# A two-layer decoder trunk: the input and the small weights handed over in the layout that the opening uses

## The chip, the cores and the metric

The kernel runs on one core of one Trainium2 chip. The metric is the device time of one execution in microseconds, as the median of several runs. The core has a matmul engine (TensorE, PE in the profile, with its weight loads shown as PEld), VectorE (DVE), ScalarE (ACT), GpSimd (POOL) and SyncE (SP). Transfers are issued from SyncE's queue, from ScalarE's and from GpSimd's, and run on 16 DMA engines.

## The reference, cut to what matters

The input is x of 512 tokens by 1024 features. Two mixer layers follow each other, each with a dense SwiGLU network behind it, and a last norm. The change touches the first mixer alone:

```python
hn = rmsnorm(h, mix_norm_g[0])                  # h is x at this point
z = gelu(hn @ w_in)                             # 1024 -> 2048
u, v = split(z, 2)
v = layernorm(v, ln_g, ln_b)                    # 4 chunks of 128 tokens, 8 groups of 128 features
w = where(causal, w_s, 0)                       # (8, 128, 128): group, target token, source token
mixed = einsum('gts,bcsgd->bctgd', w, v) + b_s
h = h + (u * mixed) @ w_out
```

All is float32. The later parts (first feed-forward network, retention, second network) are the same before and after.

## The kernel before

**Products.** A float32 value is split into a high part rounded to fp32r (ScalarE, a copy) and the low rest (VectorE, a subtraction); a product of two matrices is three fp32r matmuls (high by high, high by low, low by high), accumulated in PSUM. Most large products use seven block products instead of eight (`seven`), named P1, P7, P6, Q4, P5, P2 and P3, on sums of weight blocks and sums of activation blocks. A sum of weight blocks is made either by VectorE from two loaded tiles, or by a DMA that adds while it loads (issued by POOL); which blocks go which way is set by the arguments `dma` and `onto`.

**The opening** (lines 1407 to 1476). The left operand of a matmul has the features on the partitions, but x is stored by token. So each of eight pieces of x (128 tokens by 512 features, `load_x`) is loaded into X, turned by four TensorE transposes into PSUM (`turn_in`, lines 1265 to 1291), scaled there by the norm weight of its feature by VectorE into `xr_in`, copied to its high part `XH_in` by ScalarE and reduced to its low part `XL_in` by VectorE. The factor of the norm that depends on the token (`rc`) is put in later, where v is activated, and into R for u. The norm weights are loaded as 8 rows of 128 (`load_rows`) and turned by a transpose into a column per block (`rows_to_cols`). The first half of v's columns (`ps_v`, 96 products of 128x512) is multiplied piece by piece as the turned pieces appear (`open_step`); the weights come through `open_w`. The squares for the norm are summed by ScalarE over X.

Before that TensorE runs five wake-up matmuls on ones (`WAKE`), and a few more (`fill`) after the first turned pieces.

**The rest of the first mixer.** The second half of v's columns (`project_n("v1", ...)`, also `ps_v`), then u by seven block products in the order `UO`, among which the spatial mixing (`mix`, fp32 matmuls) is put. The spatial weights are loaded target first (`wsn`), turned by eight transposes (`wsT`), copied by VectorE and masked by POOL (`prepare_mix`, lines 1573 to 1581). Their row sums come from two fp32 matmuls with a tile of ones (`prepare_bias`, lines 1583 to 1589). The gains of the layer norm and of retention are 32 rows, turned by one transpose (`gains_ps`). The product by w_out (`so`) adds into X, and the first network (`gu`, `dn`) follows.

**Order.** No engine's order is that of the program text. Every operation is recorded with an estimated duration; a planner gives each a due time, worked back from the matmuls that need it (`backward`, `rec.ahead` moves it earlier), then simulates all engines and DMA queues forward and lets each engine take the ready operation that is due first, TensorE the ready matmul that was recorded first (`forward`). The operations are then issued in the simulated order, and each engine keeps to it. Tiles come from 39 buffers of 4 KB a partition (`G`) and eight PSUM banks. As all operations are issued by one line (377) of the recorder, the profile is read by tiles.

Of the kernel before, what the change touches and what calls it, by code (L numbers as in the profile page):

```python
# [8 lines left out]
F32 = mybir.dt.float32  # L9
# [14 lines left out]
GROUPS = 8  # L24
WAKE = 5
PREP = 5
# [10 lines left out]
U_DMA = ("P7",)  # L37
U_ONTO = ()
TABLES_AHEAD = 120000
# [630 lines left out]
@with_exitstack  # L670
def trunk(ctx, tc, x, positions, mix_g, ffn_g, fin_g, sgu_w_in, sgu_w_s, sgu_b_s, sgu_ln_g, sgu_ln_b,
          sgu_w_out, ret_w_in, ret_gn_g, ret_w_out, ffn_w_gu, ffn_w_down, invf, decay, out):
    rec = Recorder(tc)
# [83 lines left out]
    def rows_to_cols(name):
        n = rows_in[name].shape[0]
        ps = PS(f"{name}_ps", (P, 1, T))
        nc.tensor.transpose(ps[:, 0, 0:n], rows_in[name], ident[0:n, 0:n])  # L760
        cols = const.tile([P, n], F32, name=f"{name}_cols")
        nc.vector.tensor_copy(cols, ps[:, 0, 0:n])
        done(ps)
        return cols


# [495 lines left out]

    turned = {}

    def turn_in(c, j):

        ps = PS(f"xT_in_{c}_{j}", (P, 4, P))
        for k in range(4):
            turned[c, j] = nc.tensor.transpose(ps[:, k, :], X[:, c, (4 * j + k) * P:(4 * j + k + 1) * P], ident)
        if (c, j) == (0, 0):  # L1270
            xn.update(name="in", h=XT("XH_in"), l=XT("XL_in"))
        if c % 2 == 0:
            XR.setdefault(("in", c // 2), []).append(G(f"xr_in_{c // 2}_{j}", F32, (P, 4, H)))
        cs = slice(c * P, (c + 1) * P)
        for k0, n in ((0, 2), (2, 2)) if (c, j) == (0, 0) else ((0, 4),):
            ks, js = slice(k0, k0 + n), slice(4 * j + k0, 4 * j + k0 + n)
            own = XR["in", c // 2][j][:, ks, (c % 2) * P:(c % 2 + 1) * P]
            if (c, j, k0) == (0, 0, 0):
                rec.ahead = 4000
            if (c, j, k0) == (0, 0, 2):  # L1280
                for k in range(2):
                    nc.scalar.activation(own[:, k, :], ps[:, 2 + k, :], AF.Copy, scale=mix0[:, 2 + k:3 + k])
            else:
                nc.vector.tensor_tensor(own, ps[:, ks, :], mix0[:, js, None].to_broadcast([P, n, P]), ALU.mult)
            if (c, j, k0) == (0, 0, 0):
                nc.vector.tensor_copy(xn["h"][:, js, cs], own)
            else:
                nc.scalar.activation(xn["h"][:, js, cs], own, AF.Copy)
            rec.ahead = 0
            nc.vector.tensor_tensor(xn["l"][:, js, cs], own, f32(xn["h"][:, js, cs]), ALU.subtract)  # L1290
        done(ps)

    def normed(name, g, more=None):
# [122 lines left out]

    rec.ahead = 6000
    load_rows(nc.scalar, "mix0", mix_g[0:1])
    load_x(0, 0)
    load_x(1, 0)  # L1420
    rec.ahead = 0
    mix0 = rows_to_cols("mix0")
    v0w, v0r = [None] * NC, [None] * NC

    def open_w(i):
        wr = G(f"wr_v0_{i}")
        for a in range(2) if i < 2 else ():
            nc.sync.dma_start(wr[:, a, :], w_in[(2 * i + a) * P:(2 * i + a + 1) * P, D:D + T])
        if i >= 2:
            nc.sync.dma_start(wr, w_in[2 * i * P:(2 * i + 2) * P, D:D + T].rearrange("(a p) n -> p a n", p=P))  # L1430
        wh, wl = G(f"wh_v0_{i}", F32R), G(f"wl_v0_{i}", F32R)
        for at in (slice(0, 1), slice(1, 2)) if i < 2 else (slice(0, 2),):
            nc.scalar.activation(wh[:, at, :], wr[:, at, :], AF.Copy)
            nc.vector.tensor_tensor(wl[:, at, :], wr[:, at, :], f32(wh[:, at, :]), ALU.subtract)
        v0w[i] = wh, wl

    def open_step(c, i):
        wh, wl = v0w[i]
        cs = slice(c * P, (c + 1) * P)
        o = vps[c // 2][:, c % 2, :]  # L1440
        for n, (x_, w_) in enumerate((("h", wh), ("h", wl), ("l", wh))):
            for a in range(2):
                k = 2 * i + a
                nc.tensor.matmul(o, xn[x_][:, k, cs], w_[:, a, :], start=(k == 0 and n == 0), stop=(k == KD - 1 and n == 2),
                                 skip_group_check=True)

    turn_in(0, 0)
    vps = [PS(f"ps_v0_{i}") for i in range(2)]

    def fill(n, at):  # L1450
        for _ in range(n):
            rec.follow(nc.tensor.matmul(vps[1][:, 0, :], flat[:, 0, 0:P], flat[:, 0, :], start=True, stop=True), turned[at])

    fill(2, (0, 0))
    for j in range(2):
        for c in range(NC):
            if c == 0:
                open_w(2 * j)
            if (c, j) != (3, 1):
                at = (c + 1) % NC, j + (c + 1) // NC  # L1460
                if at != (1, 0):
                    load_x(*at)
            if c == 1:
                open_w(2 * j + 1)
            if (c, j) != (3, 1):
                turn_in(*at)
            if (c, j) == (0, 0):
                fill(1, at)
            open_step(c, 2 * j)
            if c == 1:  # L1470
                open_step(0, 2 * j + 1)
            if c >= 1:
                open_step(c, 2 * j + 1)
            if j == 1:
                square_in(c)
    rc = rsqrt_cols(ss2, NC, 1.0 / D, "n0")
# [72 lines left out]


    load_rows(nc.sync, "gains", ret_gn_g, sgu_ln_g, sgu_ln_b)
    gains = rows_to_cols("gains")

# [13 lines left out]
    add_b = G("add_b", F32, (P, GROUPS, P))  # L1567
    wsn = G("wsn", F32, (P, GROUPS, P))
    nc.sync.dma_start(wsn, sgu_w_s[0].rearrange("g t s -> t g s"))
    nc.sync.dma_start(add_b, sgu_b_s.rearrange("l g t -> l (g t)").to_broadcast([P, GROUPS * P]))  # L1570
    R = TMP("R0")

    def prepare_mix():
        ps = PS("wsT", (P, GROUPS, P))
        for g in range(GROUPS):
            nc.tensor.transpose(ps[:, g, :], wsn[:, g, :], ident)
        nc.vector.tensor_copy(wst, ps)
        done(ps)
        nc.gpsimd.affine_select(
            out=wst, in_=wst, compare_op=ALU.is_ge, fill=0.0, base=0,  # L1580
            pattern=[[0, GROUPS], [1, P]], channel_multiplier=-1)

    def prepare_bias():
        ps = PS("rowsum", (P, GROUPS, P))
        for j in range(2):
# [25 lines left out]

    project_n("v1", w_in, ((D + T, T),), after_v1)
    mx = [None] * KD
# [36 lines left out]
    def mix(j, half):  # L1650
        for i in (2 * half, 2 * half + 1):
# [10 lines left out]
            if i % 2 == 1:  # L1662
                done(ps)

    jobs.extend(seven("u", w_in, rows(0, KD), 0, T, uparts, gate_u,
                      {("P1", 0): prepare_bias, ("P1", 1): lambda: mix(0, 0), ("P7", 0): lambda: mix(0, 1), ("P7", 1): lambda: mix(1, 0),
# [317 lines left out]
```

## Time and profile before

| | |
|---|---|
| median of 3 runs | 1176.3 us (1176.13 to 1176.56) |
| profiled execution | 1176.45 us, span 1174.5 us |
| granted clock | 0.999 |
| PE / PEld busy | 1165.5 / 1063.8 us (99% / 91%) |
| DVE / ACT / POOL busy | 1008.8 / 695.3 / 177.5 us (86% / 59% / 15%) |
| DMA | 233.00 MB, mean 198 GB/s |

Times are microseconds from the start of the span. In a row of the timeline or the chain stand start, duration, engine, line, operation, the tile written, the tiles read and the count; in brackets the idle time before it and what ended it. A row of the waits says who waited for whom, the sum, how often and the longest. The busy time of matmuls overlaps, since they are pipelined; the distance between starts is what one costs in a stream. A row of the landing times gives the size of a load and the time from issue to landing. A row that groups instructions ends with busy time and the mean of one in ns.

### The profile page before, as it was taken

What the parts mean: (1) busy time and instruction counts of PE and PEld (TensorE: products, weight loads), DVE (VectorE), ACT (ScalarE), POOL (GpSimd) and SP (SyncE); (2) the same over time, 40 slices, a digit from 0 to 9 for tenths busy, and PEclk for the clock granted to TensorE, in tenths of its full rate; (3) what the DMA queues carried; (4) which work ended last, traced back from release to release, by engine and by line L of the source; (5) the groups of instructions that cost most, each with busy time, mean ns of one, the idle gap of its engine ahead of it and who ended that gap; (6) DMA issues with size and microseconds to landing.
All of it is one profiled execution on the core that took longest, in us unless ns stands there. A gap on an engine that the chain in (4) does not pass through costs nothing.

```text
span 1174.5 us, 18866 instructions
## 1 busy us (share of the span) xinstructions
PE 1165.5 (99%) x7492; PEld 1063.8 (91%) x7492; DVE 1008.8 (86%) x1246; ACT 695.3 (59%) x915; POOL 177.5 (15%) x153
## 2 busy tenths in 40 slices
PE   9999999999999999999999999999999999999997
PEld 7899899989999988888889898888999889999986
DVE  7999999798779899998868787899998987665896
ACT  7446876456543558767555585577675544535474
POOL 0012121211100220221111111220211111001220
PEclk9999999999999999999999999999999999999999
DMA  9458988899856898988777678887897898769892
GB/s 327 120 143 191 319 202 207 180 239 217 201 141 158 193 189 264 220 184 209 179 175 193 148 193 215 189 170 252 212 220 169 202 241 198 189 153 247 179 224 82
DMA packets 132777, 233.00 MB, mean 198 GB/s; under 512 B 7592, under 2 KB 32208, under 8 KB 132688
## 3 DMA queue, kind: packets, MB, share of 16 engines
q1 hardware_dynamic: 91152, 156.80, 40.8%
q0 software_dynamic: 41376, 74.72, 38.2%
q8 instruction: 59, 0.97, 0.3%
q10 hardware_dynamic: 160, 0.27, 0.1%
q14 instruction: 30, 0.25, 0.1%
HBM read 228.61 MB, written 2.10 MB: 196 GB/s over the span
## 4 chain that ended last, share of the span: by engine, by line
PE 98%; ACT 1%; DMA 0%; DVE 0%; SPq 0%; issue 0%; DVEq 0%
PE X_gu L377 22%; PE Y_gu L377 11%; PE X_dn L377 9%; PE X_vg L377 7%; PE Z_gu L377 5%; PE Y_dn L377 5%; PE X_qk L377 4%; PE ps_v L377 4%; PE Y_vg L377 4%; PE X_ro L377 4%; PE Z_dn L377 3%; PE pv L377 2%; PE Y_qk L377 2%; PE X_u L377 2%; PE X_so L377 2%; PE Y_ro L377 2%
## 5 line engine op out<-in xcount | busy, mean ns | idle before, releaser
L377 ACT ACTIVATE wh_gu_P<-wr_gu_P 128x1024 fp32r<-128x1024 f32 x132 | 138.6, 1061 | 119.9 <-DMA wr_gu_P<-in_ffn_w_gu 32.8
L377 DVE TENSOR_TENSOR wl_gu_P<-wr_gu_P,wh_gu_P 128x1024 fp32r<-128x1024 f32 x132 | 160.2, 1222 | 42.5 <-ACT wh_gu_P L377 29.8
L377 POOL DMA_DIRECT2D wr_gu_P<-in_ffn_w_gu x50 | 60.7, 1248 | 378.4 <-DVE wl_gu_P L377 186.0
L377 ACT ACTIVATE wh_dn_P<-wr_dn_P 128x1024 fp32r<-128x1024 f32 (+1 forms) x72 | 69.4, 984 | 44.1 <-PE Y_gu L377 12.4
L377 DVE TENSOR_TENSOR wl_dn_P<-wr_dn_P,wh_dn_P 128x1024 fp32r<-128x1024 f32 (+1 forms) x72 | 80.5, 1134 | 11.0 <-ACT wh_dn_P L377 10.6
L377 POOL DMA_DIRECT2D wr_dn_P<-in_ffn_w_down x40 | 46.3, 1203 | 172.8 <-DVE wl_dn_P L377 63.7
L377 DVE TENSOR_TENSOR wl_vg_P<-wr_vg_P,wh_vg_P 128x1024 fp32r<-128x1024 f32 x48 | 57.6, 1221 | 8.7 <-ACT wh_vg_P L377 6.3
L377 ACT ACTIVATE wh_vg_P<-wr_vg_P 128x1024 fp32r<-128x1024 f32 x48 | 49.7, 1057 | 9.5 <-PE Z_qk L377 3.5
L377 POOL DMA_DIRECT2D wr_vg_P<-in_ret_w_in x26 | 31.6, 1292 | 140.3 <-DVE wl_vg_P L377 60.4
L377 PE MATMUL Z_gu<-XH_f,wh_gu_P 128*128 128x256 f32 x176 | 50.0, 284 | 0.0
L377 PE MATMUL X_gu<-XH_f,wh_gu_P 128*128 128x256 f32 x176 | 49.9, 284 | 0.0
L377 PE MATMUL Y_gu<-xP7h_f,wh_gu_P 128*128 128x256 f32 x176 | 49.8, 283 | 0.0
L377 PE MATMUL Y_gu<-xP7l_f,wh_gu_P 128*128 128x256 f32 x176 | 49.8, 283 | 0.0
L377 PE MATMUL Y_gu<-xP7h_f,wl_gu_P 128*128 128x256 f32 x176 | 49.8, 283 | 0.0
L377 PE MATMUL X_gu<-xP6h_f,wh_gu_P 128*128 128x256 f32 x176 | 49.8, 283 | 0.0
L377 PE MATMUL X_gu<-xP6l_f,wh_gu_P 128*128 128x256 f32 x176 | 49.8, 283 | 0.0
L377 PE MATMUL X_gu<-xP6h_f,wl_gu_P 128*128 128x256 f32 x176 | 49.8, 283 | 0.0
L377 PE MATMUL X_gu<-xP5h_f,wh_gu_P 128*128 128x256 f32 x176 | 49.8, 283 | 0.0
L377 PE MATMUL X_gu<-xP5l_f,wh_gu_P 128*128 128x256 f32 x176 | 49.8, 283 | 0.0
L377 PE MATMUL X_gu<-xP5h_f,wl_gu_P 128*128 128x256 f32 x176 | 49.8, 283 | 0.0
L377 PE MATMUL Y_gu<-XH_f,wh_gu_Q 128*128 128x256 f32 x176 | 49.8, 283 | 0.0
L377 PE MATMUL Y_gu<-XL_f,wh_gu_Q 128*128 128x256 f32 x176 | 49.8, 283 | 0.0
(676 smaller groups left out, 4388.1 us busy)
## 6 DMA issues: line engine op xcount, KB each, us to landing
wr_gu_P<-in_ffn_w_gu SPq DMA_DIRECT2D x110, 512.0 KB, 5.7
wr_gu_P<-in_ffn_w_gu POOLq DMA_DIRECT2D x50, 512.0 KB, 7.5
wr_dn_P<-in_ffn_w_down SPq DMA_DIRECT2D x50, 512.0 KB, 5.1
wr_vg_P<-in_ret_w_in SPq DMA_DIRECT2D x40, 512.0 KB, 5.8
wr_dn_P<-in_ffn_w_down POOLq DMA_DIRECT2D x33, 512.0 KB, 6.9
wr_vg_P<-in_ret_w_in POOLq DMA_DIRECT2D x26, 512.0 KB, 8.1
wr_qk_P<-in_ret_w_in SPq DMA_DIRECT2D x20, 512.0 KB, 4.5
wr_ro_P<-in_ret_w_out SPq DMA_DIRECT2D x20, 512.0 KB, 5.1
```

The source lines that it names most:

```text
L377: return fn(*[real_of(a) for a in args], **{k: real_of(a) for k, a in kwargs.items()})
```

## The change

The host hands over the same numbers in other layouts: x a second time by feature (`xt`, in two halves of 256 tokens), the first norm's weights and the gains as columns, the spatial weights source first, and w_in cut into u's part and the two halves of v's. No arithmetic is done on the host.

In the kernel `load_rows`, `rows_to_cols`, `turn_in`, `fill` and the transposes in `prepare_mix` go. A piece of xt (256 features by 256 tokens) is loaded straight into `xr_in`; ScalarE writes the scaled high part, VectorE the scaled low part in one instruction, and the scaling of `xr_in` itself, which u needs later, follows by VectorE after two pieces (`gain_xt`). The first half of v is computed by halves of the tokens. X by token is still loaded, for the squares and the residual. The causal mask is a product with a triangle of ones. The row sums use fp32r matmuls on a high and a low part of the masked weights. WAKE goes from 5 to 10, and u's block product Q4 has its last weight block added by DMA (`U_ONTO`). The core of the diff, with unchanged lines left out:

```diff
-WAKE = 5
+WAKE = 10
-U_ONTO = ()
+U_ONTO = ("Q4",)
...
+    upper = const.tile([P, P], F32, name="upper")
+    nc.vector.memset(upper, 1.0)
+    nc.gpsimd.affine_select(out=upper, in_=upper, compare_op=ALU.is_ge, fill=0.0, base=0, pattern=[[1, P]], channel_multiplier=-1)
...
+    def load_xt(i, q):
+        if q % 2 == 0:
+            XR.setdefault(("in", i), []).append(G(f"xr_in_{i}_{q // 2}", F32, (P, 4, H)))
+        ks = slice(2 * (q % 2), 2 * (q % 2) + 2)
+        nc.sync.dma_start(XR["in", i][q // 2][:, ks, :], xt[i, q // 2][:, ks, :])
+
+    def split_xt(i, q):
+        own = XR["in", i][q // 2]
+        hs = slice(i * H, (i + 1) * H)
+        for k in (2 * q, 2 * q + 1):
+            nc.scalar.activation(xn["h"][:, k, hs], own[:, k % 4, :], AF.Copy, scale=mix0[:, k:k + 1])
+        for k in (2 * q, 2 * q + 1):
+            nc.vector.scalar_tensor_tensor(xn["l"][:, k, hs], own[:, k % 4, :], mix0[:, k:k + 1], f32(xn["h"][:, k, hs]),
+                                           ALU.mult, ALU.subtract)
+
+    def gain_xt(i, j):
+        own = XR["in", i][j]
+        nc.vector.tensor_tensor(own, own, mix0[:, 4 * j:4 * j + 4, None].to_broadcast([P, 4, H]), ALU.mult)
...
+    def products(i, q, alist):
+        _, wh, wl = v0w[q]
+        for n, (x_, w_) in enumerate((("h", wh), ("l", wh), ("h", wl))):
+            for a in alist:
+                k = 2 * q + a
+                for c in (2 * i, 2 * i + 1):
+                    nc.tensor.matmul(vps[i][:, c % 2, :], xn[x_][:, k, c * P:(c + 1) * P], w_[:, a, :], start=(k == 0 and n == 0),
+                                     stop=(k == KD - 1 and n == 2), skip_group_check=True)
...
+    rec.ahead = 6000
+    nc.scalar.dma_start(mix0, mix_cols)
+    load_xt(0, 0)
+    rec.ahead = 5000
+    load_w(0)
+    rec.ahead = 4000
+    load_xt(1, 0)
+    rec.ahead = 0
...
+    for q in range(1, 4):
+        load_xt(0, q)
+        load_w(q)
+        load_xt(1, q)
+        for c in {2: (0, 1), 3: (2, 3)}.get(q, ()):
+            nc.sync.dma_start(X[:, c, :], x[c * P:(c + 1) * P, :])
+        split_xt(0, q)
+        split_w(q)
+        products(0, q, (0, 1))
+        split_xt(1, q)
+        products(1, q, (0, 1))
+        if q % 2 == 1:
+            gain_xt(0, q // 2)
+            gain_xt(1, q // 2)
+        for c in {2: (0, 1), 3: (2, 3)}.get(q, ()):
+            square_in(c)
...
-    load_rows(nc.sync, "gains", ret_gn_g, sgu_ln_g, sgu_ln_b)
-    gains = rows_to_cols("gains")
+    gains = const.tile([P, 32], F32, name="gains")
+    nc.sync.dma_start(gains, gain_cols)
...
-    nc.sync.dma_start(wsn, sgu_w_s[0].rearrange("g t s -> t g s"))
+    nc.sync.dma_start(wst, sgu_w_st)
...
     def prepare_mix():
-        ps = PS("wsT", (P, GROUPS, P))
-        for g in range(GROUPS):
-            nc.tensor.transpose(ps[:, g, :], wsn[:, g, :], ident)
-        nc.vector.tensor_copy(wst, ps)
-        done(ps)
-        nc.gpsimd.affine_select(
-            out=wst, in_=wst, compare_op=ALU.is_ge, fill=0.0, base=0,
-            pattern=[[0, GROUPS], [1, P]], channel_multiplier=-1)
+        nc.vector.tensor_tensor(wst, wst, upper[:, None, :].to_broadcast([P, GROUPS, P]), ALU.mult)
...
     def prepare_bias():
         ps = PS("rowsum", (P, GROUPS, P))
-        for j in range(2):
-            nc.tensor.matmul(ps[:, 4 * j:4 * j + 4, :], ones, wst[:, 4 * j:4 * j + 4, :], start=True, stop=True)
+        wsh, wsl = G("wsh", F32R, (P, GROUPS, P)), G("wsl", F32R, (P, GROUPS, P))
+        nc.scalar.activation(wsh, wst, AF.Copy)
+        nc.vector.tensor_tensor(wsl, wst, f32(wsh), ALU.subtract)
+        for q in (wsh, wsl):
+            for j in range(2):
+                nc.tensor.matmul(ps[:, 4 * j:4 * j + 4, :], onesr, q[:, 4 * j:4 * j + 4, :], start=(q is wsh), stop=(q is wsl),
+                                 skip_group_check=True)
```

More of the change, by code (lines that the diff above doesn't have):

```diff
@@ L670, in trunk @@
 @with_exitstack
-def trunk(ctx, tc, x, positions, mix_g, ffn_g, fin_g, sgu_w_in, sgu_w_s, sgu_b_s, sgu_ln_g, sgu_ln_b,
-          sgu_w_out, ret_w_in, ret_gn_g, ret_w_out, ffn_w_gu, ffn_w_down, invf, decay, out):
+def trunk(ctx, tc, x, xt, positions, mix_cols, mix_g, ffn_g, fin_g, sgu_w_u, sgu_w_v, sgu_w_st, sgu_b_s, gain_cols,
+          sgu_w_out, ret_w_in, ret_w_out, ffn_w_gu, ffn_w_down, invf, decay, out):
     rec = Recorder(tc)
@@ L1261, in turn @@
         return ps
[L1263 to L1291, printed above, removed]
     def normed(name, g, more=None):
@@ new lines, in trunk, with load_w, split_w @@
+    v0w = []
+    def load_w(q):
+        wr = G(f"wr_v0_{q}")
+        if q < 2:
+            for a in range(2):
+                nc.sync.dma_start(wr[:, a, :], sgu_w_v[0, (2 * q + a) * P:(2 * q + a + 1) * P, :])
+        else:
+            nc.sync.dma_start(wr, sgu_w_v[0, 2 * q * P:(2 * q + 2) * P, :].rearrange("(a p) n -> p a n", p=P))
+        v0w.append((wr, G(f"wh_v0_{q}", F32R), G(f"wl_v0_{q}", F32R)))
+    def split_w(q):
+        wr, wh, wl = v0w[q]
+        for at in (slice(0, 1), slice(1, 2)) if q < 2 else (slice(0, 2),):
@@ L1433, in open_w @@
             nc.scalar.activation(wh[:, at, :], wr[:, at, :], AF.Copy)
             nc.vector.tensor_tensor(wl[:, at, :], wr[:, at, :], f32(wh[:, at, :]), ALU.subtract)
[L1435 to L1445, printed above, removed]
@@ L1447, in trunk @@
-    turn_in(0, 0)
-    vps = [PS(f"ps_v0_{i}") for i in range(2)]
[L1450 to L1454, printed above, removed]
-    for j in range(2):
[L1456 to L1475, printed above, removed]
+    def products(i, q, alist):
[6 more added lines that the diff above has]
+                                     stop=(k == KD - 1 and n == 2), skip_group_check=True)
@@ new lines, in trunk @@
+    xn.update(name="in", h=XT("XH_in"), l=XT("XL_in"))
+    mix0 = const.tile([P, KD], F32, name="mix0")
+    rec.ahead = 6000
[6 more added lines that the diff above has]
+    rec.ahead = 0
+    vps = [PS(f"ps_v0_{i}") for i in range(2)]
+    split_xt(0, 0)
+    split_w(0)
+    products(0, 0, (0,))
+    products(0, 0, (1,))
+    split_xt(1, 0)
+    products(1, 0, (0,))
+    products(1, 0, (1,))
+    for q in range(1, 4):
[14 more added lines that the diff above has]
+            square_in(c)
@@ L1610, in turn_tables @@
         next(rotary, None)
-    project_n("v1", w_in, ((D + T, T),), after_v1)
+    project_n("v1", sgu_w_v[1], ((0, T),), after_v1)
     mx = [None] * KD
@@ L1663, in mix @@
                 done(ps)
-    jobs.extend(seven("u", w_in, rows(0, KD), 0, T, uparts, gate_u,
+    jobs.extend(seven("u", sgu_w_u, rows(0, KD), 0, T, uparts, gate_u,
                       {("P1", 0): prepare_bias, ("P1", 1): lambda: mix(0, 0), ("P7", 0): lambda: mix(0, 1), ("P7", 1): lambda: mix(1, 0),
@@ L1954, with _laid_out, cols @@
         "sgu_ln_b", "sgu_w_out", "ret_w_in", "ret_gn_g", "ret_w_out", "ffn_w_gu", "ffn_w_down"]
+def _laid_out(a):
+    import numpy as np
+    def cols(*gs):
+        return np.ascontiguousarray(np.concatenate([g.reshape(-1, P) for g in gs]).T)
+    x = a["x"].reshape(T, D)
+    w_in = a["sgu_w_in"].reshape(D, 2 * D)
+    return {
+        "x": x,
+        "xt": np.ascontiguousarray(x.reshape(2, T // 2, 2, 4, P).transpose(0, 2, 4, 3, 1)),
+        "positions": a["positions"],
+        "mix_cols": cols(a["mix_norm_g"][0]),
+        "mix_norm_g": a["mix_norm_g"], "ffn_norm_g": a["ffn_norm_g"], "final_norm_g": a["final_norm_g"],
+        "sgu_w_u": np.ascontiguousarray(w_in[:, :D]),
+        "sgu_w_v": np.ascontiguousarray(w_in[:, D:].reshape(D, 2, T).transpose(1, 0, 2)),
+        "sgu_w_st": np.ascontiguousarray(a["sgu_w_s"][0].transpose(2, 0, 1)),
+        "sgu_b_s": a["sgu_b_s"],
+        "gain_cols": cols(a["ret_gn_g"], a["sgu_ln_g"], a["sgu_ln_b"]),
+        "sgu_w_out": a["sgu_w_out"], "ret_w_in": a["ret_w_in"], "ret_w_out": a["ret_w_out"],
+        "ffn_w_gu": a["ffn_w_gu"], "ffn_w_down": a["ffn_w_down"],
+    }
 def _constants():
@@ L1973 @@
     nc = bacc.Bacc("TRN2", target_bir_lowering=False, num_devices=1, dynamic_dma_scratch_size=4096)
-    arrays = {n: np.ascontiguousarray(inputs[n]) for n in _INS}
-    arrays["x"] = arrays["x"].reshape(T, D)
-    arrays |= _constants()
+    arrays = _laid_out({n: np.ascontiguousarray(inputs[n]) for n in _INS}) | _constants()
     arrays = {f"in_{n}": a for n, a in arrays.items()}
```

37 lines of the change are left out of this document (removed).

## The prediction

> **What bounds the kernel now.** I read the page first, then TensorE's waits, then the chain of waits for the opening, then the timeline of the first 12 us.
>
> ```profile
> span 1174.5 us, 18866 instructions
> PE 1165.5 (99%) x7492; PEld 1063.8 (91%) x7492; DVE 1008.8 (86%) x1246; ACT 695.3 (59%) x915; POOL 177.5 (15%) x153
> PE wake L377 <- DVE flat L377: 1.5, 1, 1.5
> PE ps_v L377 <- ACT wh_v L377: 0.4, 2, 0.2
> ```
>
> The last two rows are all the waits that TensorE has in the whole run. Once it has started it never stands still, so the time is the moment of a dense start plus the TensorE work behind it plus a tail. A microsecond of matmul taken out is a microsecond won, as long as the others keep up.
>
> ```profile
> 1.73 5.14 DMA wr_v<-in_sgu_w_in
> 9.58 4.98 PE ps_v L377 x21
> 14.56 0.44 PE xT_in L377 x4
> ...
> 27.35 0.44 PE xT_in L377 x4
> 27.79 10.48 PE ps_v L377 x46
> 38.26 0.17 PE gains_ps L377
> 55.95 0.87 PE wsT L377 x8
> 61.88 1.72 PE rowsum L377 x4
> 106.11 5.47 PE X_so L377 x24
> ```
>
> In the chain of waits TensorE is dense from 9.58. One fp32r product of 128x512 costs 10.48/46 = 0.228 us. By the counts of that view 189 of the 192 products of v stand behind 9.58, so three were done; a dense start would have been at 9.58 - 3 x 0.23 = 8.9.
>
> **The change, part by part: TensorE behind the start.** Five groups of four input transposes lie in the dense stretch (the first at 14.56, the last at 27.35): 5 x 0.44 = 2.2 us. The turn of the gains is 0.17, the eight turns of the spatial weights 0.87. The row sums go from two fp32 products (four records, 1.72) to four fp32r products: 4 x 0.228 = 0.91, which wins 0.81. All of it is on the path: 2.2 + 0.17 + 0.87 + 0.81 = 4.05 us. The products themselves (96 in the first half of v, 64 of mix, all of u) keep their number and form.
>
> **The start.** Timeline of TensorE, then landing times of single loads:
>
> ```profile
> 1.53 2.50 PE L377 MATMUL wake<-flat 128*128 128x512 f32 x5 [1.53 <-DVE flat L377]
> 6.63 0.78 PE L377 MATMUL ps_v<-flat 128*128 128x512 f32 x1
> 8.69 0.39 PE L377 MATMUL ps_v<-wl_v,XH_in 128*128 128x512 f32 x1
> 0.81 0.87 SPq L377 DMA_DIRECT2D X<-in_x  x2
> X<-in_x SPq DMA_DIRECT2D x2, 256.0 KB, 3.0
> 6.89 0.63 ACT L377 ACTIVATE wh_v<-wr_v 128x512 fp32r<-128x512 f32 x1 [3.96 <-DMA wr_v<-in_sgu_w_in]
> ```
>
> Before, two quarters of x go first, the first weights are third in SyncE's queue and land at 1.73 + 5.14 = 6.87; ScalarE splits them (0.63) and the first product can go at 7.5. Afterwards the due times put one piece of xt first and the weights second. The load that was second landed within 3.0 us of its issue at about 1.26, the third at 6.87: the weights land between 4.3 and 6.9, the product could go between 4.9 and 7.5. The wake-up goes from five to ten matmuls: five took 2.50, so ten end by 1.53 + 5.0 = 6.5, and they hold TensorE in order. I take 6.5, nearer to the second load's row, since the weights now are that load. A lone 128x512 matmul took 0.78 at 6.63 and 0.39 at 8.69, so the slow clock lasts to about 7.4; two products at 0.5 fit before it, and the dense start is 7.4 - 2 x 0.23 = 6.9, **2.0 us** before 8.9. The ends: 6.1 if the clock is full when the products begin (2.8 won), 8.0 if the weights land at 6.9 and the halves trickle in (0.9 won).
>
> The Trainium skill (TensorE: Matmul & The Clock Gate, Part 1: The HAM clock gate) says that about 3.4 us of sustained work release the clock and that the window runs freely. From 1.53 that would be 4.9, which the 0.78 at 6.63 does not show; by the rule the products start at full speed and the sum would be 0.5 us better.
>
> **The column of gains** (mix_cols) is now 128 runs of 32 bytes instead of 8 of 512, and the split of xt waits for it. The nearest row is inv, 128 runs of 4 bytes:
>
> ```profile
> 19.63 3.84 SPq L377 DMA_DIRECT2D add_b<-in_sgu_b_s  x1
> 23.52 0.42 SPq L377 DMA_DIRECT2D inv<-in_invf  x1
> add_b<-in_sgu_b_s SPq DMA_DIRECT2D x1, 512.0 KB, 13.6
> inv<-in_invf SPq DMA_DIRECT2D x1, 0.5 KB, 9.9
> ```
>
> It landed at 33.4, 0.2 us after the load ahead of it (33.2). So the column costs 0 to 0.2 us on its own queue, and it has until 6.5 less two scaled copies: nothing.
>
> The Trainium skill (DMA: Bandwidth & Descriptors, Specifications) asks for at least 512 bytes a run, below which the engine reads, modifies and writes. It gives no price for 128 runs; the row above shows none worth a term.
>
> **Data behind the start.** x now comes twice: 2 MB more.
>
> ```profile
> 10.00:15.00 5.00, 5.00 (x25) 4.14 (x25) 2.88 (x6) 4.21 (x7) 0.00 (x0) 1.00 1.03 388
> 35.00:40.00 5.00, 5.00 (x23) 3.86 (x22) 5.00 (x7) 2.01 (x2) 0.00 (x0) 1.00 0.23 81
> ```
>
> (Columns: stretch, then PE, PEld, DVE, ACT, POOL, clock, DMA share, GB/s.) DMA is full to 30 us and then not. 2 MB at 388 GB/s is 5.4 us. A quarter step of v now needs 1 MB in 24 x 0.228 = 5.5 us, about 190 GB/s, half of what comes; the second half's weights, needed from 6.9 + 96 x 0.228 = 28.8, have 6 MB ahead of or in them at most, which 388 GB/s bring by 4 + 15.5 = 20. Cost nothing; the cover is the 9 us between. Without it, 5.4.
>
> **VectorE** is the engine that could take the gain back, being full here.
>
> ```profile
> 106.00:220.00 114.00, 113.98 (x804) 107.02 (x804) 108.06 (x133) 79.77 (x111) 20.58 (x17) 1.00 0.89 222
> 6.10 0.42 DVE L377 TENSOR_TENSOR XL_in<-xr_in,XH_in 128x256 fp32r<-128x256 f32 x1
> L377 DVE TENSOR_TENSOR XL_in<-xr_in,XH_in 128x512 fp32r<-128x512 f32 (+1 forms) x9 | 5.7, 629 | 0.7 <-ACT XH_in L377 0.7
> L377 DVE TENSOR_TENSOR xr_in<-xT_in,mix_cols 128x512 f32<-128x512 f32 (+1 forms) x8 | 5.2, 654 | 2.3 <-PE xT_in L377 2.3
> 48.02 1.22 DVE L377 TENSOR_TENSOR wr_u_P<-wr_u_P,wr_u_Q 128x1024 f32<-128x1024 f32 x1
> 58.10 0.68 DVE L377 COPY wst<-wsT 128x512 f32<-128x512 f32 x1
> 183.03 1.22 DVE L377 TENSOR_TENSOR wl_gu_Q<-wr_gu_P,wh_gu_Q 128x1024 fp32r<-128x1024 f32 x1
> 188.24 5.76 PE Y_gu L377 x48
> ```
>
> Opening: 5.7 + 5.2 = 10.9 go; 16 fused scale-and-subtract of 128x256 (no row of this form; as the 0.42 of the subtract of that size) and 4 gains of 128x1024 at 1.22 come: 6.7 + 4.9 = 11.6, +0.7. Spatial weights: two copies go (1.37), the mask product and the low half come (2.44), +1.1. u: its Q4 block now is added by DMA (U_ONTO), so two additions of 1.22 go, -2.4. Together about 0.6 us less, where TensorE's demand comes 6 us sooner. What absorbs it is the lead: wl_gu_Q was ready at 184.25 for a product at 188.24, 4.0 us ahead, the smallest I found for weights in this full stretch; and the 2.3 us that VectorE waited for transposes go. 4.0 + 0.6 + 2.3 = 6.9 against 6.05, too near to call free. I charge 0.3 us for single waits (0 to 2).
>
> ScalarE gets 16 scaled copies of 128x256 in place of 8 copies of 128x512, each between half of 0.63 and all of it: 5.0 to 10.1 us for 5.0. At 59% busy, and 2.01 of 5.00 at 35 us, it takes the rest there; were it not idle then, the weight splits behind would be up to 5 us later.
>
> **Sum.** 4.05 + 2.0 - 0.3 = 5.75. The profiled execution took 1176.45 (span 1174.5 and 1.95 around it), which gives 1170.7; the median shown is 0.15 lower, so **1170.5 us**. Own range 1169.2 to 1172.0. All behind 106 us is only moved forward.
>
> **Rivals.** (a) *VectorE becomes the bound* until 210 us: if none of its idle comes back, the gain is lead plus saved work, 4.0 + 0.6 = 4.6, and if the order made anew leaves half the lead, 2.6: 1171.7 to 1173.7, say 1172.8. For: 108.06 of 114 busy. Against: no waits now, and 2.3 us of waiting go.
>
> (b) *Late first data*: loads land as the third did, head start 0 to 0.9: 1176.3 - 4.05 - 0.5 + 0.3 = 1172.0. For: 5.14 against 3.0 for similar loads. Against: fewer bytes are ahead.
>
> (c) *Slower, through POOL's queue.* U_ONTO puts two adding loads on it, each waiting for VectorE's low half of P6; what stands behind is the adds for so.
>
> ```profile
> wr_u_P<-in_sgu_w_in POOLq DMA_DIRECT2D x1, 512.0 KB, 10.0
> 50.29 1.22 DVE L377 TENSOR_TENSOR wl_u_P<-wr_u_P,wh_u_P 128x1024 fp32r<-128x1024 f32 x1
> 79.81 1.20 POOL L377 DMA_DIRECT2D wr_so_P<-in_sgu_w_out  x1 [19.12 <-PE mix L377]
> 107.43 1.22 DVE L377 TENSOR_TENSOR wl_so_P<-wr_so_P,wh_so_P 128x1024 fp32r<-128x1024 f32 x1
> 117.02 5.44 PE X_so L377 x24
> ```
>
> If both go out only when so's adds are due (79.81), those are late by 2 x 10.0; the lead at so's P6 is 117.02 - 108.65 = 8.4, so TensorE waits 11.6 and the kernel takes 1176.3 - 5.75 + 11.6 = 1182. It decides once they leave after about 79.8 + 8.4 - 20 + 5.75 = 74. Against: P6's low halves were done by 51.5.
>
> (d) *It doesn't do what it says*: the transposes were in gaps. The chain has them inside the dense stretch; only 3 of 8 groups lay before it. 1176.
>
> **Chances.** Forecast 0.62, (a) 0.17, (b) 0.08, (c) 0.08 with any like it, (d) 0.05. The range runs from 1168.8 (head 2.8, no waits, 0.6 for faster landings) to 1173.8, which takes in (a) and (b). 0.2% (2.4 us) is what a measurement can tell: faster 0.86, same 0.06, slower 0.08.
>
> **What would show it.** Right: no xT_in, gains_ps or wsT rows; rowsum near 0.9; first ps_v product near 6.5, dense soon after; X_so at 106.11 - 6 = 100; waits of TensorE still under 1 us. Wrong: PE waits on DVE between 80 and 210 (a), first product after 7.5 (b), PE X_so or Y_so waiting on a wr_so load (c).

## The result, and the profile after

The changed kernel takes 1170.63 us (median of five runs, 1170.24 to 1172.29), the kernel before 1176.56 (five runs, 1176.13 to 1178.01) beside it. The ratio is 0.9948 with a 95% interval of 0.9938 to 0.9959: about 5.9 us faster. The forecast was 1170.5.

The page of the changed kernel:

```profile
span 1170.6 us, 18792 instructions
PE 1159.7 (99%) x7452; PEld 1060.3 (91%) x7452; DVE 1008.0 (86%) x1245; ACT 696.9 (60%) x922; POOL 177.5 (15%) x155
PE 91%; DVE 6%; ACT 1%; DMA 1%; issue 0%; DVEq 0%
```

All waits of TensorE in it (sum, times, longest):

```profile
PE X_gu L377 <- ACT u L377: 1.6, 1, 1.6
PE wake L377 <- DVE flat L377: 1.5, 1, 1.5
PE X_so L377 <- DVE y_P3l L377: 0.3, 1, 0.3
PE X_u L377 <- DVE usP L377: 0.3, 1, 0.3
```

Forty TensorE records are gone (7492 to 7452). VectorE has 0.8 us less to do, ScalarE 1.6 more. A wait of 1.6 us is new, and with it this profiled execution is the slowest of the five (1172.29; the others end between 1170.24 and 1170.67). The last line shown is the page's chain of work that ended last: 6% of the span in it are VectorE's. Before, 98% of that chain were TensorE's.

The timeline of the opening, first ScalarE, then TensorE:

```profile
3.72 0.91 ACT L377 ACTIVATE XH_in<-xr_in,mix 128x256 fp32r<-128x256 f32 x2 [0.97 <-DMA mix<-in_mix_cols]
4.54 1.27 ACT L377 ACTIVATE wh_v<-wr_v 128x512 fp32r<-128x512 f32 x2
```

```profile
1.53 4.63 PE L377 MATMUL wake<-flat 128*128 128x512 f32 x10 [1.53 <-DVE flat L377]
5.96 1.05 PE L377 MATMUL ps_v<-wh_v,XH_in 128*128 128x512 f32 x2
6.81 0.70 PE L377 MATMUL ps_v<-wh_v,XL_in 128*128 128x512 f32 x2
7.35 0.63 PE L377 MATMUL ps_v<-wl_v,XH_in 128*128 128x512 f32 x2
```

The column of gains has landed by 3.72, the weights by 4.54, and the ten wake-ups give way to the first product at 5.96. Pairs start 0.85 apart at first, and behind 7.35 the single products follow each other at 0.23, half the distance: read from this distance, TensorE's clock went to full speed, or opened, at about 7. The granted clock in the windows of the profile reads 1.00 from the start of the opening on and doesn't show it, so here and below the moment is inferred from the spacing.

The chain of waits between the end of v and the first network, changed kernel (start, duration, what):

```profile
49.16 1.22 DVE wl_u_P L377
...
92.89 0.61 DVE usP L377
...
93.54 6.02 PE X_u L377 x48
99.56 5.47 PE X_so L377 x24
...
134.55 1.15 DVE y_P3l L377
```

`X_so` starts at 99.56 where it started at 106.11: 6.55 us are won by then. But from 49.16 to 92.89 every piece of the chain is VectorE's or an issue between two of its instructions. TensorE is busy in that stretch too, and at its end waits 0.3 us for VectorE: the two are about level, and which of them sets the end of u is a question for the experiments. How full VectorE is there shows in the busy time by stretches, first of the kernel before, then of the changed one (columns as in the prediction: PE, PEld, DVE, ACT, POOL):

```profile
49.00:93.00 44.00, 44.00 (x336) 41.71 (x335) 41.60 (x70) 20.80 (x25) 4.24 (x4) 1.00 0.50 133
```

```profile
49.00:93.00 44.00, 44.00 (x364) 43.48 (x362) 43.55 (x71) 21.44 (x26) 5.24 (x5) 1.00 0.70 170
```

Of 44 us VectorE was idle 2.4 before and 0.45 after. The same work lies some 6 us later in the kernel before; from 55.2 to 99.2 VectorE was idle 1.7 there. That is where the prediction's "too near to call" was decided.

The new 1.6 us wait, in the chain of the changed kernel:

```profile
164.19 12.52 DMA wr_gu_P<-in_ffn_w_gu
...
176.73 1.06 ACT wh_gu_P L377
177.78 0.49 ACT u L377
```

A weight load took 12.52 us to land; the page's two rows for this weight have medians of 5.0 us from SyncE's queue and 7.1 from GpSimd's. ScalarE did its split first, `u` stood behind it, and TensorE waited for `u` until 178.32.

### The profile page after: what moved, and what is told of

The parts are those of the page before. It is cut to its first block, busy times and chain, and to the rows that moved or that the text cites. A ratio compares the mean times of both kernels' runs of the same rounds, so it can differ in the third digit from the quotient of the medians.

```text
span 1170.6 us, 18792 instructions
## 1 busy us (share of the span) xinstructions
PE 1159.7 (99%) x7452; PEld 1060.3 (91%) x7452; DVE 1008.0 (86%) x1245; ACT 696.9 (60%) x922; POOL 177.5 (15%) x155
## 4 chain that ended last, share of the span: by engine, by line
PE 91%; DVE 6%; ACT 1%; DMA 1%; issue 0%; DVEq 0%
PE X_gu L377 21%; PE Y_gu L377 10%; PE X_dn L377 9%; PE X_vg L377 7%; PE Y_dn L377 5%; PE Z_gu L377 5%; PE X_qk L377 4%; PE Y_vg L377 4%; PE X_ro L377 4%; PE ps_v L377 4%; PE Z_dn L377 3%; PE pv L377 2%; PE Y_qk L377 2%; PE Y_ro L377 2%; PE Z_vg L377 2%; PE X_so L377 1%
## 5 line engine op out<-in xcount | busy, mean ns | idle before, releaser
L377 PE MATMUL X_gu<-xP3l_f,wh_gu_P 128*128 128x256 f32 x176 | 49.8, 283 | 0.0
L377 PE MATMUL X_gu<-xP3h_f,wl_gu_P 128*128 128x256 f32 x176 | 49.8, 283 | 0.0
```

Source lines behind the costliest of these rows:

```text
L377: return fn(*[real_of(a) for a in args], **{k: real_of(a) for k, a in kwargs.items()})
```

## The experiments

Two theories stood against each other. By the first, TensorE's own path sets the time as the prediction's sum has it, and what is lost besides is single waits. By the second, VectorE's lead is used up, so its work and the moment at which it gets its data decide. The theories A and B of the single expectations are others from run to run. The ratios are against the kernel before on the same chip (1176.56, 1176.51 and 1176.33 us in the three groups of runs).

To place a gain or a loss, this table has starts on TensorE, read from its timeline, as us earlier than before (the last product of v, of u and of so, then the 200th and 400th product of the first network's `gu`; the last is the last of the kernel):

| kernel | v | u | so | gu 200 | gu 400 | last |
|---|---|---|---|---|---|---|
| changed, first profile | 5.31 | 6.55 | 5.60 | 5.72 | 3.86 | 3.88 |
| changed, again | 5.00 | 6.24 | 5.33 | 5.45 | 5.44 | 5.46 |
| scaling on ScalarE | 6.40 | 6.20 | 6.38 | 6.37 | 6.37 | 6.35 |
| more VectorE work | 3.98 | 5.62 | 4.78 | 4.76 | 4.75 | 4.58 |
| without `U_ONTO` | 5.44 | 6.40 | 3.65 | 3.77 | 1.60 | 1.62 |
| five wake-ups | 4.31 | 5.54 | 4.60 | 4.72 | 4.70 | 4.71 |
| 2 MB more loaded | 5.69 | 6.39 | 2.31 | 2.41 | -1.25 | -1.25 |
| spatial part as before | 6.05 | 4.75 | 4.94 | 4.94 | 4.94 | 4.95 |
| late loads, ScalarE, nine wake-ups | 6.29 | 6.43 | 6.61 | 6.60 | 6.60 | 5.61 |

Two things make single differences in it less than they seem. The clock opened at other moments in the single profiles, between 4.7 and 7.7 us where nothing interrupts the wake-ups, and that alone moves the end of v by 1.4 us between runs 1 and 2. And in the rows of runs 2, 7 and 12 two products of so, 0.45 us together, stand ahead of the last products of u, so that column reads 0.45 too low there.

**1. The changed kernel again**, with no edit (an empty diff).

> The changed kernel once more, unaltered, as the base for the others of this call. In its first profile TensorE waited 1.6 us at 176.7 for a split behind a late adding load of the first feed-forward network, and that execution (1172.29) was 1.7 above the median of its runs (1170.63). Theory A (that wait is chance in one execution, the order is the same): the new profile lacks it, the span is near 1169, the advance against the kernel before stays near 5.5 us behind 180 us instead of 3.9. Theory B (the wait belongs to the order, since the lead is used up): it stands in the new profile too, with 1 to 2 us.

Measured: 1170.61 us (1170.02 to 1170.68), ratio 0.9947 (0.9933 to 0.9962). All waits of TensorE behind the wake-up:

```profile
PE X_so L377 <- DVE y_P3l L377: 0.3, 1, 0.3
PE X_u L377 <- DVE usP L377: 0.3, 1, 0.3
```

The load that took 12.52 us landed in 8.1 here: the 1.6 us wait was chance, and cost what that profile stood above the rest. The span is 1169.0, and the table's second row is the one to read the change by: 5.00 won at the end of v, 6.24 at the end of u, 0.8 given back by gu's 200th product, none after it. The new profile is as theory A has it.

**2. The scaling of `xr_in` on ScalarE.**

```diff
-        nc.vector.tensor_tensor(own, own, mix0[:, 4 * j:4 * j + 4, None].to_broadcast([P, 4, H]), ALU.mult)
+        for k in range(4 * j, 4 * j + 4):
+            nc.scalar.activation(own[:, k % 4, :], own[:, k % 4, :], AF.Copy, scale=mix0[:, k:k + 1])
```

> The later scaling of xr_in (four VectorE products of 128x1024, 1.22 us each) is done by 16 scaled ScalarE copies of 128x256 instead, about 0.45 us each. VectorE has 4.6 us less to do before 20 us, ScalarE 7 us more. Theory A (VectorE has just enough lead, and the few waits at 130 to 180 come from it): waits of TensorE behind 80 us go down from about 0.6 to 0.3 or less, time 1169.5 to 1170.6. Theory B (VectorE is the bound until 210 us and holds back the gain): 2 us or more faster than the changed kernel. Theory C (nothing hangs on it): same within 0.5 us.

Measured: 1169.89 us (1169.62 to 1170.07), ratio 0.9942 (0.9926 to 0.9959), 0.7 less than the changed kernel in the same runs. In its profile v ended 1.4 us sooner, since the clock opened at 4.7 here, and u ended no sooner: TensorE waited instead.

```profile
PE rowsum L377 <- DVE R L377: 0.8, 1, 0.8
```

With the two products of so counted, u was done about 0.4 us sooner for a v that ended 1.4 sooner: in that stage VectorE holds back most of a better head start of TensorE. The rest of the gain came behind it: the 0.8 us are not given back at so. The time lies in theory A's range. Of the four scalings taken from VectorE (1.22 each) one had lain inside the full stretch, at 72.38 in the changed kernel.

**3. Four more operations of VectorE in the opening**, each a maximum of a scaled piece with itself, which changes no value (4 x 1.22 us).

```diff
         nc.vector.tensor_tensor(own, own, mix0[:, 4 * j:4 * j + 4, None].to_broadcast([P, 4, H]), ALU.mult)
+        nc.vector.tensor_tensor(own, own, own, ALU.max)
```

> Four more VectorE operations of 128x1024 in the opening, in place, each the maximum of a tile with itself (about 1.14 us in a stream, 4.6 us in all), before u needs them. The result stays the same. Theory A (a lead of some 2 to 4 us is left behind the change): 0 to 2.6 us slower than the changed kernel. Theory B (VectorE is the bound): slower by the whole 4.6. Theory C (VectorE has much room): no difference.

Measured: 1171.85 us (1171.62 to 1171.90), ratio 0.9959 (0.9944 to 0.9974), 1.25 more than the changed kernel. It looks like a price of VectorE's work, and the trace says otherwise. Timeline of TensorE:

```profile
18.23 1.19 PE L377 MATMUL ps_v<-wh_v,XH_in 128*128 128x512 f32 x4 [1.57 <-ACT wh_v L377]
```

The chain that leads to it:

```profile
8.67 8.43 DMA wr_v<-in_sgu_w_v
...
17.12 1.06 ACT wh_v L377
```

In the order made anew the four loads of X (5.03 to 7.99 in SyncE's queue) went ahead of one more weight load, which then left at 8.67 and landed at 17.10, late for TensorE. v ends 1.0 us later than in run 1 and the kernel 0.9, so the loss lies in the opening. The wait costs more than that, but the clock opened at 5.4 here and at 7.7 in run 1, which gives some of it back. Three of the four added operations lie before 49 us, where VectorE had idle time, one at 75.8. The time lies in theory A's range, but for another reason. The run is no clean test of the work it added; it shows that the loads of the second x can make TensorE wait when the order puts them ahead of a weight load.

**4. Without `U_ONTO`**, all else as changed.

```diff
-U_ONTO = ("Q4",)
+U_ONTO = ()
```

> The changed kernel with u's last weight block added by VectorE as before (U_ONTO empty): two VectorE additions of 1.22 us come back in the u stage and two adding loads leave GpSimd's queue. Theory A (VectorE has just enough lead): 0 to 1.5 us slower, with waits of TensorE between 80 and 210 us. Theory of the prediction's rival c (the adding loads delay so): faster, with Y_so or X_so no longer waiting. If neither: same within 0.5 us.

Measured: 1174.09 us (1173.52 to 1174.67, ten runs), ratio 0.9978 (0.9968 to 0.9987): 3.5 us more, for two additions of 1.22 us. Waits of TensorE behind the wake-up, the longest four:

```profile
PE X_gu L377 <- ACT wh_gu_P L377: 1.1, 1, 1.1
PE X_u L377 <- DVE usP L377: 0.6, 1, 0.6
PE X_gu L377 <- DVE wl_gu_P L377: 0.5, 1, 0.5
PE Y_so L377 <- ACT y_P7h L377: 0.3, 1, 0.3
```

u ends as early as with it, then 2.75 us are lost at so and 2.05 more in gu. VectorE is behind throughout; one operation that all these kernels have (timeline of VectorE, run 1, then this run):

```profile
79.51 1.21 DVE L377 SCALAR_TENSOR_TENSOR xP3l_in<-xP_in,xP3h_in 128x1024 fp32r<-128x1024 f32 x1
```

```profile
82.47 1.21 DVE L377 SCALAR_TENSOR_TENSOR xP3l_in<-xP_in,xP3h_in 128x1024 fp32r<-128x1024 f32 x1
```

It comes 3.0 us later, and the kernel takes 3.5 more. Three operations more lie between the layer norm and this one, 1.13 each in a stream: the two additions, and one low part of u's weights that run 1 has done at 49.47 and this order does later; the stretch itself begins 0.44 sooner. Idle time is a rough measure of all this:

```profile
49.00:93.00 44.00, 44.00 (x363) 43.45 (x361) 42.83 (x69) 20.75 (x24) 3.57 (x3) 1.00 0.50 144
```

VectorE is idle 1.2 us in that window here, more than with the change, but all of it before 55, 0.7 of it waiting for v; from 55 to 93 it never stands still. One constant carries 3.5 of the 5.9 us. Theory A had 0 to 1.5 for it, with VectorE's lead just enough; the run says that the lead is not enough without `U_ONTO`.

**5. Five wake-ups again.**

```diff
-WAKE = 10
+WAKE = 5
```

> The changed kernel with five wake-up matmuls instead of ten. The wake-up then ends near 4.0 us and TensorE stands until the first split weights at 5.2; the first product can go 0.7 us sooner (5.95 with ten). Theory A (the clock opens some 5 to 6 us after the first matmul and the pause does not put it off): 0 to 0.4 us faster than the changed kernel. Theory B (the pause puts the full clock off by several us): the products of the first quarter run at twice their 0.23 for longer, 1 to 2 us slower.

Measured: 1171.35 us (1170.78 to 1171.88), ratio 0.9958 (0.9943 to 0.9973). Timeline of TensorE:

```profile
5.30 1.22 PE L377 MATMUL ps_v<-wh_v,XH_in 128*128 128x512 f32 x2 [1.27 <-ACT wh_v L377]
...
8.88 1.00 PE L377 MATMUL ps_v<-wh_v,XL_in 128*128 128x512 f32 x2
9.72 0.62 PE L377 MATMUL ps_v<-wl_v,XH_in 128*128 128x512 f32 x2
```

The weights let the first product go at 5.30, 0.66 sooner than ten wake-ups do, but the products stay slow until 9.7, against 7.0 and 7.7 in the two profiles of the changed kernel. Net 0.7 us worse, between the two expectations. The longer wake-up helps, as it seems by bridging the pause; that the pause and not the number of matmuls counts was not separated.

**6. 2 MB more to load in the opening**: x by token is loaded a second time into the same tile.

```diff
             nc.sync.dma_start(X[:, c, :], x[c * P:(c + 1) * P, :])
+            nc.sync.dma_start(X[:, c, :], x[c * P:(c + 1) * P, :])
```

> The changed kernel with each of the four loads of x by token issued twice: 2 MB more in the opening, into the same tiles. Theory A (the prediction: the second layout of x costs nothing, the data run some 9 us ahead): same within 0.5 us. Theory B (transfers are the limit of the opening): up to 5.4 us slower, with TensorE waiting for wh_v or wl_v in the second half of v.

Measured: 1177.19 us (1175.18 to 1177.56, ten runs), ratio 1.0002 (0.9992 to 1.0011). The whole gain is gone, 6.6 us, and TensorE never waited in v: v and u end as early as with the change. Neither theory had that. What waited was ScalarE, and VectorE behind it. Timeline of ScalarE, then waits of VectorE between 8 and 30 us:

```profile
18.75 1.06 ACT L377 ACTIVATE wh_v<-wr_v 128x1024 fp32r<-128x1024 f32 x1 [5.16 <-DMA wr_v<-in_sgu_w_v]
```

```profile
DVE wl_v L377 <- ACT wh_v L377: 4.6, 2, 3.7
```

Run 1 has 1.7 us of waits in that window (1.1 and 0.6). VectorE does not make this up (timeline of VectorE):

```profile
83.62 1.22 DVE L377 SCALAR_TENSOR_TENSOR xP3l_in<-xP_in,xP3h_in 128x1024 fp32r<-128x1024 f32 x1
```

That is 4.1 us later than in run 1. The weights of u left SyncE's queue at 22.82 instead of 18.86, and four operations on them that run 1 has done before the layer norm stand behind it here. TensorE pays at so and gu: `X_so` waits 1.2 and `mix` 0.6 on VectorE's `mx`, and the 1.1, 0.5 and 0.3 of run 4 are there too. Of the loss in this profile, 1.5 us are of another kind: after two pauses in gu the clock fell. The window has a mean granted clock of 0.91 (the first number behind POOL), and the chain shows a slower gu:

```profile
180.00:200.00 20.00, 20.00 (x156) 20.00 (x155) 18.24 (x20) 10.28 (x12) 3.49 (x3) 0.91 0.85 203
```

```profile
179.58 9.91 PE X_gu L377 x68
```

Without `U_ONTO` (run 4) the same products behind the same two waits, at full clock:

```profile
178.22 8.42 PE X_gu L377 x68
```

Without these 1.5 us the price is 5.1, for a VectorE that is 4.1 late, as run 4's 3.5 was for 3.0. Whether the clock fell in the other nine executions isn't known.

**7. The spatial weights and row sums as before**, the rest as changed.

```diff
-    nc.sync.dma_start(wst, sgu_w_st)
+    wsn = G("wsn", F32, (P, GROUPS, P))
+    nc.sync.dma_start(wsn, sgu_w_st)
...
-        nc.vector.tensor_tensor(wst, wst, upper[:, None, :].to_broadcast([P, GROUPS, P]), ALU.mult)
+        ps = PS("wsT", (P, GROUPS, P))
+        for g in range(GROUPS):
+            nc.tensor.transpose(ps[:, g, :], wsn[:, g, :], ident)
...
-        "sgu_w_st": np.ascontiguousarray(a["sgu_w_s"][0].transpose(2, 0, 1)),
+        "sgu_w_st": np.ascontiguousarray(a["sgu_w_s"][0].transpose(1, 0, 2)),
```

> The changed kernel with the spatial weights loaded target first, turned by eight transposes, masked on GpSimd and summed by two fp32 matmuls as before; x by feature, the gains as columns, the wake-up and U_ONTO stay. TensorE has 0.87 + 0.81 = 1.7 us more to do, VectorE 1.1 us less, ScalarE 1.05 less. Theory A (TensorE's work decides): 1.2 to 1.8 us slower than the changed kernel. Theory B (VectorE is the bound there): 0.5 us slower or less, or faster.

Measured: 1171.42 us (1170.53 to 1171.95), ratio 0.9958 (0.9942 to 0.9975). TensorE has 1.68 us more to do (the terms 0.87 and 0.81), u ends 1.5 us later than in run 1 (1.0 with the two products of so counted), and the time is only 0.8 longer, between the two theories: nothing is given back behind u, and one wait remains (`X_u` on `usP`, 0.6). So the two terms are worth 0.8 of 1.68. In this profile v ended 1.05 us sooner than in run 1, since the clock opened at 5.5; how much of the missing half is that, and how much VectorE's lateness in the changed kernel, this run doesn't tell.

**8. `U_ONTO` alone**, put into the kernel before.

```diff
-U_ONTO = ()
+U_ONTO = ("Q4",)
```

> The kernel before with one line changed: u's last weight block is added by DMA (U_ONTO as in the changed kernel). VectorE loses two additions of 1.22 us. Theory A (before, VectorE's lead sufficed and TensorE never waited; the line is worth something only where TensorE comes sooner): same as before within 0.5 us. Theory B (the line is a gain of its own): 2 to 3.5 us faster than before, as much as it was worth in the changed kernel.

Measured: 1176.64 us (1175.55 to 1177.83, ten runs), ratio 1.0002 (0.9992 to 1.0011): nothing. VectorE did get the time (window):

```profile
49.00:93.00 44.00, 44.00 (x336) 41.72 (x335) 39.27 (x68) 19.08 (x23) 5.18 (x5) 1.00 0.61 154
```

41.60 became 39.27, the two additions, and no one waited for it: before, VectorE had idle time in this stretch. With run 4 this is what tells the theories apart: taking out the same two additions is worth nothing in the kernel before, where VectorE stands idle 2.4 us in this window, and 3.5 us in the changed one, where with them gone it stands idle 0.45.

**9. The loads of x by token due 8 us later.**

```diff
+            rec.ahead = -8000
             nc.sync.dma_start(X[:, c, :], x[c * P:(c + 1) * P, :])
+            rec.ahead = 0
```

> The changed kernel with the due time of the four loads of x by token moved 8 us later, so that SyncE issues them behind all four weight loads of the first half of v instead of ahead of two of them. The bytes are the same. After the doubled load cost 6.6 us at 100 to 190 us while v itself never waited, Theory A is: what the second x costs is VectorE's lead, not TensorE's data; with the weights first VectorE stands less between 15 and 20 us, the waits at 130 us go, 0.3 to 0.9 us faster than the changed kernel (1169.7 to 1170.3). Theory B (only the sum of bytes counts): same within 0.2.

Measured: 1170.53 us (1169.67 to 1170.66), ratio 0.9944 (0.9931 to 0.9958): no change. The edit hardly did what it says:

```profile
7.20 2.52 SPq L377 DMA_DIRECT2D X<-in_x  x4
```

They left at 7.20 instead of 6.52, behind one weight load more. Theory B's number came out, but the run doesn't test it. Whether a load that is really late would help stays open.

**10. Late loads and the scaling on ScalarE** (runs 2 and 9 together).

```diff
-        nc.vector.tensor_tensor(own, own, mix0[:, 4 * j:4 * j + 4, None].to_broadcast([P, 4, H]), ALU.mult)
+        for k in range(4 * j, 4 * j + 4):
+            nc.scalar.activation(own[:, k % 4, :], own[:, k % 4, :], AF.Copy, scale=mix0[:, k:k + 1])
...
+            rec.ahead = -8000
             nc.sync.dma_start(X[:, c, :], x[c * P:(c + 1) * P, :])
+            rec.ahead = 0
```

> The later loads of x by token together with the later scaling of xr_in on ScalarE (which alone gave 1169.89). Theory A (both feed the same lead, and what is left to win is only the last waits of TensorE, 1.0 us in that run): 1169.2 to 1169.9. Theory B (they add up): 1169.0 or less.

Measured: 1170.28 us (1169.82 to 1170.39), ratio 0.9945 (0.9932 to 0.9957). The loads left at 9.84 this time, and nothing added up: no gain over run 2, and slower than either theory had it.

**11. Scaling on ScalarE, the causal mask on GpSimd** instead of VectorE's product with `upper`. The scaling is changed as in run 2; the lines of the mask:

```diff
-    upper = const.tile([P, P], F32, name="upper")
-    nc.vector.memset(upper, 1.0)
-    nc.gpsimd.affine_select(out=upper, in_=upper, compare_op=ALU.is_ge, fill=0.0, base=0, pattern=[[1, P]], channel_multiplier=-1)
...
-        nc.vector.tensor_tensor(wst, wst, upper[:, None, :].to_broadcast([P, GROUPS, P]), ALU.mult)
+        nc.gpsimd.affine_select(
+            out=wst, in_=wst, compare_op=ALU.is_ge, fill=0.0, base=0,
+            pattern=[[0, GROUPS], [1, P]], channel_multiplier=-1)
```

> The scaling of xr_in on ScalarE and the causal mask back on GpSimd as in the kernel before (one operation of 1.08 us there), which takes another 1.14 us from VectorE. Theory A (VectorE's lead is no longer short once the scaling is on ScalarE): same as the ScalarE version (1169.89) within 0.3. Theory B (VectorE still short): 0.5 us faster or more.

Measured: 1170.97 us (1170.18 to 1172.44), ratio 0.9953 (0.9941 to 0.9966): about 1 slower than run 2 although VectorE has one operation less. The mask lies before 49 us, where VectorE has idle time, and the order is another. Neither theory had it slower, and a difference of 1 us between two orders is not explained further here.

**12. Run 10 with nine wake-ups.**

```diff
-WAKE = 10
+WAKE = 9
```

> The later loads and the scaling on ScalarE with nine wake-up matmuls instead of ten. The ninth ends 0.43 us sooner, when the first split weights are just there (about 5.2 to 5.4), so TensorE does not pause. Theory A (a pause is what put the full clock off with five): 0 to 0.3 us faster than with ten. Theory B (the number of wake-up matmuls is what counts): slower.

Measured: 1169.84 us (1169.66 to 1170.53), ratio 0.9943 (0.9931 to 0.9955). Timeline of TensorE, and its longest waits behind the wake-up:

```profile
5.47 0.62 PE L377 MATMUL ps_v<-wh_v,XH_in 128*128 128x512 f32 x2
```

```profile
PE X_gu L377 <- ACT u L377: 0.8, 1, 0.8
PE rowsum L377 <- DVE R L377: 0.5, 1, 0.5
```

The first product goes at 5.47 and at full clock. v ends 6.29 us sooner than before and u 6.43: with the two products of so counted, about 0.6 of the 1.3 us that v ends sooner than in run 1 reach the end of u. One us is lost at 205 us to the wait on `u`, which stood on ScalarE behind the split of a weight load as in the first profile; this execution, too, is the slowest of its five. Runs 2 and 12 are the fastest, 0.7 to 0.8 us below the changed kernel, with intervals that overlap its own. No clearly better version was found.

## Why the prediction was right, and where it was not

**The sum.** Predicted 5.75 us, measured 5.5 in spans (1174.5 to 1169.0 in run 1) and 5.9 in medians. But its parts did not all hold, and that they cancelled is luck: in run 1 the head start was 2.6 us instead of 2.0, and the loss behind v 1.2 (5.00 + 1.68 - 5.46) instead of 0.3.

**TensorE behind the start, 4.05.** Right as work. No transposes of x, of the gains or of the spatial weights are left, and the row sums' four products, with the row for the high part and the row for the low one, start between 53.3 and 54.1:

```profile
L377 PE MATMUL rowsum<-wsh,onesr x2: 398/422/446, 53.3 to 53.6; 128*128 128x512 f32 x2
L377 PE MATMUL rowsum<-wsl,onesr x2: 392/394/397, 53.9 to 54.1; 128*128 128x512 f32 x2
```

0.8 from first to last and 0.23 for the last make about 1.0, against 0.91. As gain, the 1.68 us for the spatial weights and the row sums came to 1.24 at the end of u (6.24 - 5.00) and to 0.8 in the time (run 7).

**The start, 2.0.** Too small. At the end of v 5.00 us were won, of which 2.37 is the transposes and the turn of the gains: the head start was 2.6 (2.9 in the first profile). Two steps were off. Ten wake-ups were put at twice the time of five, 6.5, and gave way at 5.96, since starts behind the first are 0.43 apart and only the last one's end counts in full; and "the slow clock lasts to about 7.4" was one moment where the runs have many: about 7.0 and 7.7 in the two profiles of the changed kernel. The good end, with the clock full when the products begin, was put at 6.1; runs 2 and 12 had it, with the first product at 5.39 and 5.47.

The Trainium skill (TensorE: Matmul & The Clock Gate, Part 1: The HAM clock gate) has the clock released by a window of activity of about 3.4 us that runs freely, so that the moment varies. The prediction held 4.9 against the trace, and run 2 opened at 4.7; the moments found, 3.1 to 6.1 us after the first wake-up, agree with a free window better than with the fixed 7.4 taken, but are spread wider than the 0.5 us either way that the section gives.

**Single waits, -0.3.** Measured 0.3 + 0.3 in run 1, and 0.8 given back from u to gu. This is rival (a) in small.

**VectorE: half of rival (a).** The total was right, 0.6 us less predicted and 0.8 on the page, though the fused scale-and-subtract takes more than the 0.42 taken from the subtract:

```profile
L377 DVE SCALAR_TENSOR_TENSOR XL_in<-xr_in,mix,XH_in x16: 475/476/486, 4.3 to 22.8; 128x256 fp32r<-128x256 f32 x16
```

The step that failed is where the lead was looked for. "4.0 us ahead, the smallest I found" was taken for weights at 188; the place that became tight is 49 to 136, where VectorE's work hangs on the results of u. "The 2.3 us that VectorE waited for transposes" lie in the opening, while the layer norm and most work on u begin only once v is done; no run moved them alone, so that they didn't help is argued, not shown. What counted is how much of u's work VectorE has done before the layer norm and how long it still stands idle behind it: from 49 to 93 that idle time was used up. Rival (a)'s price, 1171.7 to 1173.7, was not paid because `U_ONTO` took its two additions out of this very stretch. The prediction carried that edit as a term of -2.4 in VectorE's total; run 4 shows it as 3.5 us in the time of the changed kernel. Without it the kernel takes 1174.1, outside the range.

The Trainium skill (Perfetto Trace Analysis, Identifying the Most-Contended Engine and Optimization Strategy) names the most occupied engine as the one to work on, TensorE judged by its weight loads rather than its matmuls, and adds that this can change between regimes. The occupancy alone doesn't settle it here: between 49 and 93 TensorE is busy 44.00 of 44 us, its weight loads 43.48, VectorE 43.55. That VectorE's work counts there is shown by runs 2 and 4.

**The second x, "cost nothing; the cover is the 9 us between".** That TensorE doesn't wait for it in v holds in run 1. What the second x costs in all was not measured, since no run leaves it out. The argument failed in two places. The 6 MB leave out 2: x twice and both halves of v's weights are 8 MB, which by the same rate land at 4 + 21.6 = 25.6, not 20. In run 1 the last of these loads, issued at 16.21, took 9.4 us and landed at 25.6; the cover was 3 us up to 28.8, not 9. And the cover was worked out for TensorE alone. The transfers' second consumer, VectorE, has none: 2 MB more cost 6.6 us with TensorE never waiting in v (run 6), 5.1 without the fall of the clock, near the 5.4 that the prediction gave as the bare price. And in another order a weight load behind the four loads of X made TensorE itself wait 1.57 (run 3). "5.4 without cover" should have been a bound of the range with a price per consumer.

**The column of gains** cost nothing, as said: ScalarE waited 0.97 for it at 3.72 and TensorE was in its wake-ups until 5.96.

**The other rivals.** (b), late data, is refuted by a first product at 5.96. (c) is refuted in its sign: without the adding loads through GpSimd's queue the kernel is 3.5 us slower (run 4), and no so product waits on a load. (d) is refuted by the end of v.

## What to carry to other kernels

Where the matmul engine never waits, work taken out of it counts one for one only as far as the next engine's idle time reaches, and that has to be measured in the stretch where its inputs come from the matmuls just moved, not over the span and not at the smallest lead found elsewhere. Idle time is only a first sign of it; what the engine has done ahead of that stretch counts as well (run 4). An extra transfer that is hidden from the matmul engine is not hidden from the engine that is full behind it: work out the cover for each consumer. A side edit that frees time on the second engine can be worth nothing by itself and still be most of the gain beside another edit, so it is tried in both kernels.

## What was not expected of the hardware

**When the clock opens.** In eleven profiles whose wake-ups run into the products without a pause, the spacing of TensorE's starts falls from 0.43 to 0.23 us somewhere between 4.7 and 7.7 us, at other moments in two executions of one kernel (7.0 and 7.7). In run 2 the change falls among the wake-ups themselves, which are all the same instruction on the same tile. The granted clock of the windows reads 1.00 on both sides of the change (first profile of the changed kernel, runs 2 and 5); only the spacing tells. With a pause of 1.27 us behind the wake-ups it was 9.7 (run 5, one profile).

**When it falls.** In run 6 two gaps between starts of 1.41 and 0.79 us within 2.7 us were followed by 3.4 us at about half pace (starts 0.21 apart instead of 0.12, from 180.3 to 183.7; granted clock 0.91 over 180 to 200), 1.5 us lost; in run 4 the same two gaps were followed by none. So here two pauses cost most of their length again in one execution, and nothing in another. The Trainium skill (TensorE: Matmul & The Clock Gate, Part 1: The HAM clock gate) gives the slow clock after an idle window of about 3.4 us; here gaps of 2.2 us in all came before it, in one of two executions, and the slow stretch lasted those 3.4.

**Landing times.** One weight load of 12.52 us, against medians of 5.0 and 7.1 for such loads, cost 1.6 us in one execution of the changed kernel; in the next the same load took 8.1 and nothing waited.
